# A diffusion-transformer step on one core: the activation arena as sixteen tensors, early products P1 ahead of P2, and a modulation moved to TensorE

## The chip, the cores and the metric

The kernel runs on one core of one Trainium2 chip. The metric is device time in microseconds (us) of one execution. A run has one number, and a kernel's time is the median of its runs.

## The reference, cut to what matters

One inference step with two layers (DEPTH = 2), D = 1024, 1024 sample tokens and 128 context tokens, all in float32. Each layer normalises x, modulates it with a scale and a shift, projects it into three parallel branches (a convolution, grouped-query attention, neighbourhood attention), projects the branches back, and then runs a squared-ReLU MLP with 4096 hidden features.

```python
def _modulation(cvec, w, b):
    m = (jax.nn.silu(cvec) @ w + b)[:, None, :]
    return jnp.split(m, 6, axis=-1)

def _layer(x, mod, lw, ctx):
    sh1, sc1, g1, sh2, sc2, g2 = mod
    h = _rms(x, n1) * (1 + sc1) + sh1
    ...                                   # h @ w_in, convolution, two attentions
    x = x + g1 * (jnp.concatenate([a_out, b_out, c_out], axis=-1) @ w_out)
    h = _rms(x, n2) * (1 + sc2) + sh2
    x = x + g2 * (jnp.square(jax.nn.relu(h @ w1)) @ w2)
```

The modulation is `silu(c) @ ada_w + ada_b`, with ada_w of 1024 x 6144, for two conditioning vectors. The next layer's first third (shift and scale of its first norm) is needed when that layer begins.

## The kernel before, in words

Activations are kept feature by feature: a block has 128 features on the partitions and tokens along the row. The 1152 tokens are two halves of HT = 576 (512 sample and 64 context tokens each). Every float32 operand of a large matmul is split into a rounded part `hi` and a rest `lo`, and a product is the three matmuls hi*hi, hi*lo, lo*hi (`three`, L1369, on two PSUM banks of 288 columns).

**The arena.** One region of on-chip memory, 16 x 1152 words a partition, holds activations in split form, and at other times raw weights. It is one tensor under two names: `HA` (the type of split operands) and `HF` (plain float32). The order of all work is written out by hand, and a tile framework places the semaphores from the accesses it sees, so that an instruction waits for those before it whose data it needs or overwrites. Uses of the arena, in order: in the prologue, ada_w and half of the sample (HF); the normalised input `h` of a layer's first half (HA, `h_views`); the three branches' outputs (HA, `c_block`, `c_put`); the MLP's operands B11, B21, T2, B22 and T1 (HA, `ha`, `block`), with the plain difference `raw` (HF) on the place where T2's `lo` comes; and the weights w2, in four regions A12, A11, A22, A21 (HF, `w2`, `load2`).

**The MLP's first product** is done by a seven-product scheme (Winograd's form of Strassen's) on 2 x 2 blocks. The hidden features come in 16 groups g; a group has the products P1 to P7, of 24 matmuls each. P1 = A11*B11 and P2 = A12*B21 need only tokens of the first half, so for g < EARLY = 8 they run in an *early stage*, while VectorE and ScalarE still prepare the second half (`norm2(L, 1, norms)`, stepped by `next(pre)` once or twice after each product). P1 and P2 of an early group accumulate in the same two banks `psa`: ScalarE copies P1 out (`s1`), then P2 is added and read out as h11 = relu(...)^2. Both are stored in `sd`. The *main stage* then runs P6, P5, P7, P3, P4 for the early groups and all seven for the others. The hidden values go to memory (`hd`), through `stores` and `keep(n)`, which issues all but the last n.

w1 blocks are loaded by `load1` (256 KB each) into T tiles, combined by `sums1`, and split by `split1`; `prepare(x + 1)`, `prepare(x + 2)` do that two products ahead. All loads and stores are issued on SyncE's (SP) queue in the order of the program. T tiles number 18, S tiles (X, `ev`, `low`, `hi34` and others) 18, U tiles 19, PSUM banks 8.

**Around it.** `out_proj` makes the output projection in blocks n of 128 features, first tokens' half t = 0, then t = 1. It stores x (`dy`) through its own `keep`, runs `norm2` of the first half in between, and calls `M.begin`, which loads and splits the first w1 blocks. In the last group (g = 15), w2 loads are issued after each product from P2 on. Then come the steps of the second product: each takes `ti` (two hidden blocks, loaded from `hd`), and splits it and a w2 block.

**The next layer's first modulation.** In layer 0, `modulation_beside` runs beside the main stage as `fill`, stepped after every second product: VectorE multiplies and accumulates ada_w with the two conditioning vectors (tiles `macc`), and TensorE only sums over partitions. The other modulations (`modulation`) use TensorE: per 128 input features four matmuls with two columns of weights, into four strips of one bank `psmod`, and in the end four transposes (`psmt`).

At the end of layer 0, the next layer's first norm writes `h` into the arena (partly from GpSimd) beside the last w2 steps, which read HF.

Of the kernel before, what the change touches and what calls it, by code (L numbers as in the profile page):

```python
# [31 lines left out]
EARLY = 8  # L32
# [13 lines left out]
def hybrid_step(ctx, tc, I, O, depth=DEPTH):  # L46
# [23 lines left out]
    def h_views():  # L70

        return {si: tuple(HA[:, o:o + KT * SEGS[si][1]].rearrange("p (k c) -> p k c", k=KT) for o in two)
                for si, two in enumerate(((4096, 8192), (0, 12288), (16384, 17408)))}

    def c_block(x, kt):

        return HA.rearrange("p (r x k c) -> p x k r c", r=2, x=2, k=KT)[:, x, kt]
# [33 lines left out]
    HA, HF = (nc.alloc_sbuf_tensor_at(n, [128, 16 * NT], dt, offset=ARENA)[:, :] for n, dt in (("HA", F32R), ("HF", F32)))  # L111
# [68 lines left out]
    def modulation(l, groups, first=False):  # L180
# [4 lines left out]
        def fetch():  # L185
            if todo:
                r, k = todo.pop(0)
                cols = slice(r * 2048, (r + 1) * 2048)
                if first:
                    if k % 2 == 0:  # L190
                        o = {0: 0, 2: 12288, 4: 4096, 6: 8192}[k]
                        aw = HF[:, o:o + 4096].rearrange("p (a b) -> p a b", a=2)
                        ready.extend([aw[:, 0], aw[:, 1]])
                    load(ready[-2 + k % 2], I["ada_w"][l, k * 128:(k + 1) * 128, cols])
                    return
# [16 lines left out]
        for r in groups:  # L212
# [4 lines left out]
            for k in range(KT):  # L217
                aw = ready.pop(0)
                for j in range(4):
                    a = aw[:, j * 512:(j + 1) * 512] if first else aw[j]  # L220
                    mm(ps[32 * j:32 * j + 2, :], silc[:, k, :], a, start=(k == 0), stop=(k == KT - 1))
                if not first:
                    fetch()
                yield
# [16 lines left out]
            yield  # L241

    def modulation_beside(l, rs):

        todo = [(r, k, b) for r in rs for k in range(KT) for b in range(2)]
        ready = []

        def fetch():
            if todo:
                r, k, b = todo.pop(0)  # L250
                aw = T([512], n="aw")
                c = r * 1024 + b * 512
                load(aw, I["ada_w"][l, k * 128:(k + 1) * 128, c:c + 512])
                ready.append(aw)

        fetch()
        fetch()
        yield
        for r in rs:
            acc = [T([2, 256], n="macc") for _ in range(4)]  # L260
            for k in range(KT):
                for b in range(2):
                    aw = ready.pop(0)
                    for j in range(2):
                        x = aw[:, j * 256:(j + 1) * 256]
                        for s in range(2):
                            a = acc[2 * b + j][:, s, :]
                            if k == 0:
                                ts(a, x, silc[:, k, s:s + 1], ALU.mult)
                            else:  # L270
                                stt(a, x, silc[:, k, s:s + 1], a, ALU.mult, ALU.add)
                    fetch()
                    yield
            ps = P("psmod")
            nc.vector.memset(ps, 0.0)
            for _ in range(3):
                yield
            for j in range(4):
                mm(ps[32 * j:32 * j + 1, :], ones[:, 0:1], acc[j].rearrange("p s c -> p (s c)"), start=True, stop=True)
            mt = T([512], n="mt")  # L280
            nc.vector.tensor_copy(mt, ps)
            yield
            pt = P("psmt")
            for b in range(4):
                nc.tensor.transpose(pt[:, b * 128:(b + 1) * 128], mt[:, b * 128:(b + 1) * 128], ident)
            ptv = pt.rearrange("p (s b j x) -> p s j b x", s=2, b=2, j=4, x=32)
            for s in range(2):
                tt(mod[l][:, s, r * 8:(r + 1) * 8].rearrange("p (j b) -> p j b", j=4), ptv[:, s, :, :, 0],
                   ada_b(l)[:, r * 8:(r + 1) * 8].rearrange("p (j b) -> p j b", j=4), ALU.add)
                if r in (1, 4):  # L290
                    a, g = ((A1, n1g), (A2, n2g))[r == 4]
                    stt(a[l][:, s, :], mod[l][:, s, r * 8:(r + 1) * 8], 1.0, g(l), ALU.add, ALU.mult)
            yield
# [41 lines left out]
    def norm_out(parts, hi, lo):  # L335

        late = None
        for k in range(KT):
            way, jobs, c = NORM_WAYS[k], [], 0
            for si, rb, A, B in parts:  # L340
                n = SEGS[si][1]
                t = (T if n > 128 else U)([n], n="nx")
                jobs.append((t, hi[:, k, c:c + n], lo[:, k, c:c + n], xs(k, si), rb, A[:, k:k + 1], B[:, k:k + 1], partial(like, si)))
# [48 lines left out]
    def prologue(pr):  # L392
# [10 lines left out]
        xh = HF[:, 8192:12288].rearrange("p (a b) -> p a b", a=4)  # L403
        for i in range(4):
            load(xh[:, i, :], I["x_sample"][(i + 4) * 128:(i + 5) * 128, :])
# [1598 lines left out]
```

## Time and profile before

| what | value |
|---|---|
| median of 3 runs | 3122.18 us (3115.1 to 3123.33) |
| the profiled execution's own time | 3122.03 us |
| its span, first to last instruction | 3120.3 us |
| mean granted TensorE clock | 0.959 |
| busy: TensorE / VectorE / ScalarE / GpSimd | 92% / 68% / 45% / 21% |
| early stage, layer 0 and layer 1 | 754.5 to 849.2 us, 2307.7 to 2402.6 us |
| last five products of w1, layer 0 and layer 1 | 1161.7 to 1198.1 us, 2695.9 to 2731.0 us |

PE is TensorE, PEld its weight loads, DVE VectorE, ACT ScalarE, POOL GpSimd, SP SyncE (here: the queue that issues DMAs). In rows of waits, the first name is the engine that sat idle with the tile it was about to write, and behind the arrow stands what ended the wait; then total us, count, longest. In rows of groups, a count follows the x, then busy us and mean ns of one, then idle us just before them. In the timeline the start and the duration come first, and idle time before the row stands in brackets. In rows of stretches: start and end, length, then busy us of each engine with the number of its instructions, the granted clock, the DMA engines' share and GB/s. Most instructions are recorded in helpers: L97 is `tt` (VectorE, or GpSimd), L94 is `acopy` (ScalarE), L91 is `act`, L100 is `stt`, L141 is `load`.

### The profile page before, as it was taken

Reading aid. Unit: us, or ns where it says so; the run is one execution under the profiler, and the core shown is the slowest. Engines: PE = TensorE matmul, PEld = TensorE weight load, DVE = VectorE, ACT = ScalarE, POOL = GpSimd, SP = SyncE. Lnnn points to the kernel's source line nnn. Section 1 sums busy time; section 2 is a strip of 40 time slices with the busy share of each in tenths; the row PEclk is TensorE's granted clock in tenths of the full one; section 3 lists DMA queues with packets and bytes.
Section 4 is the critical chain, followed back from the end, with each engine's and each line's share of the span. In section 5 each row is a group of like instructions: output and inputs, shape, how many; then the busy total and the mean of one; then the engine's idle time right before and its main releaser. Section 6 shows DMA issues by size and latency. Waiting matters only on the chain.

```text
span 3120.3 us, 52813 instructions
## 1 busy us (share of the span) xinstructions
PE 2881.6 (92%) x20284; PEld 2561.1 (82%) x20284; DVE 2132.6 (68%) x4113; ACT 1395.5 (45%) x2864; POOL 655.6 (21%) x595
## 2 busy tenths in 40 slices
PE   6998999998799997999889998999988999889999
PEld 4888645898699987999878785458977999879998
DVE  6587777845687763858575877778466766376576
ACT  4334366844444443333452343568344444334343
POOL 3576256300000000000225762563000000000000
PEclk7999999999899998999989998999998999999999
DMA  7377202333465547453433670033333654374434
GB/s 274 95 193 196 66 16 77 89 106 108 135 216 194 170 145 258 131 168 96 129 127 94 186 218 31 16 96 90 103 111 128 197 179 142 121 259 164 131 99 160
DMA packets 422974, 430.42 MB, mean 138 GB/s; under 512 B 119873, under 2 KB 299841, under 8 KB 421697
## 3 DMA queue, kind: packets, MB, share of 16 engines
q1 hardware_dynamic: 422720, 427.04, 43.8%
q8 instruction: 160, 2.62, 0.3%
q14 instruction: 94, 0.76, 0.1%
HBM read 298.50 MB, written 128.45 MB: 137 GB/s over the span
## 4 chain that ended last, share of the span: by engine, by line
PE 72%; DVE 14%; DMA 5%; ACT 4%; issue 2%; POOL 2%; SPq 1%; DVEq 0%; ACTq 0%; POOLq 0%
PE ps L1369 20%; PE psa L1369 9%; PE psc L1369 6%; PE pso L1369 5%; PE psb L1369 5%; PE psacc L1168 3%; PE pspv L1035 2%; PE pspt L1019 2%; PE pst L591 2%; DVE cacc L100 2%; PE pst L592 2%; PE pst L593 2%; PE psst L1182 2%; PE psm L1094 1%; PE psd L1369 1%
## 5 line engine op out<-in xcount | busy, mean ns | idle before, releaser
L1369 PE MATMUL ps<-ts,w2h 128*128 128x288 f32 x3584 | 634.6, 299 | 43.5 <-ACT w2h L94 32.4
L1369 PEld LDWEIGHTS ps<-ts,w2h 128*128 128x128 f32 x3584 | 532.0, 191 | 50.0 <-ACT w2h L94 39.5
L1369 PE MATMUL ps<-ts,w2l 128*128 128x288 f32 x1792 | 386.4, 297 | 3.4 <-DVE w2l L97 3.4
L94 ACT CAST ts<-ti 128x576 fp32r<-128x576 f32 x256 | 172.2, 673 | 324.5 <-PE ps L1369 204.7
L591 PE MATMUL pst<-wh,HA 128*128 128x256 f32 x1040 | 297.5, 286 | 0.0
L1369 PEld LDWEIGHTS ps<-ts,w2l 128*128 128x128 f32 x1792 | 290.9, 191 | 4.3 <-DVE w2l L97 4.2
L592 PE MATMUL pst<-wl,HA 128*128 128x256 f32 x1040 | 293.9, 283 | 0.0
L593 PE MATMUL pst<-wh,HA 128*128 128x256 f32 x1040 | 293.6, 282 | 0.0
L1369 PE MATMUL psa<-HA,w1h 128*128 128x288 f32 x1024 | 200.1, 320 | 66.4 <-DVE HF L97 32.2
L91 ACT ACTIVATE ev<-ev 128x576 f32<-128x576 f32 x192 | 131.9, 687 | 253.6 <-DVE ev L97 250.6
L97 DVE TENSOR_TENSOR ts<-ti,ts 128x576 fp32r<-128x576 f32 x256 | 195.9, 765 | 68.3 <-ACT ts L94 68.3
L100 DVE SCALAR_TENSOR_TENSOR X<-ps,mod,X 128x288 f32<-128x288 f32 x336 | 112.1, 409 | 172.4 <-PE ps L1369 172.4
L1369 PEld LDWEIGHTS psa<-HA,w1h 128*128 128x128 f32 x1024 | 166.2, 207 | 76.7 <-DVE HF L97 33.5
L591 PEld LDWEIGHTS pst<-wh,HA 128*128 128x128 f32 x1040 | 198.1, 190 | 19.1 <-issue 7.8
L97 POOL TENSOR_TENSOR nacc<-nacc,nsq 128x512 f32<-128x512 f32 (+1 forms) x12 | 18.9, 1577 | 889.0 <-ACT nsq L91 889.0
L593 PEld LDWEIGHTS pst<-wh,HA 128*128 128x128 f32 x1040 | 198.4, 191 | 0.0
L592 PEld LDWEIGHTS pst<-wl,HA 128*128 128x128 f32 x1040 | 198.3, 191 | 0.1
L1793 POOL COPY yu<-X 128x128 f32<-128x128 f32 x8 | 5.6, 719 | 898.3 <-ACT ts L94 861.4
L1369 PE MATMUL pso<-HA,woh 128*128 128x288 f32 x1024 | 177.3, 295 | 0.0
L1096 DVE TENSOR_REDUCE mx<-psm 128x1 f32<-128x384 f32 x288 | 142.3, 547 | 33.6 <-PE psm L1094 33.5
L91 ACT ACTIVATE pt<-psst 128x512 f32<-128x512 f32 x216 | 118.4, 597 | 94.5 <-PE psst L1183 93.6
L97 DVE TENSOR_TENSOR w1l<-w1r,w1h 128x512 fp32r<-128x512 f32 x128 | 87.0, 689 | 105.1 <-ACT w1h L94 105.1
(283 smaller groups left out, 7108.5 us busy)
## 6 DMA issues: line engine op xcount, KB each, us to landing
ti<-hd SPq DMA_DIRECT2D x128, 576.0 KB, 3.9
hd<-ev SPq DMA_DIRECT2D x224, 288.0 KB, 3.7
aw<-in_ada_w SPq DMA_DIRECT2D x160, 256.0 KB, 4.0
w1r<-in_mlp_w SPq DMA_DIRECT2D x160, 256.0 KB, 4.1
HF<-in_mlp_w SPq DMA_DIRECT2D x128, 256.0 KB, 4.4
ddA<-o SPq DMA_DIRECT2D x144, 128.0 KB, 3.0
wr<-in_w_in SPq DMA_DIRECT2D x28, 512.0 KB, 4.1
qd<-ddA SPq DMA_DIRECT2D x48, 256.0 KB, 3.4
```

What stands on the lines that cost most here:

```text
L91: nc.scalar.activation(out=out, in_=in_, func=func, scale=scale, bias=bias, **k)
L94: nc.scalar.copy(out, in_)
L97: (eng or nc.vector).tensor_tensor(out=out, in0=a, in1=b, op=op)
L100: nc.vector.scalar_tensor_tensor(out=out, in0=a, scalar=s, in1=b, op0=op0, op1=op1)
L591: mm(o, hi, wh, start=(k == 0), stop=False)
L592: mm(o, hi, wl, start=False, stop=False)
L593: mm(o, lo, wh, start=False, stop=(k == KT - 1))
L1019: nc.tensor.transpose(ps[0:n, c], self.p[j][:, o:o + n], ident)
L1035: mm(ps[64 * j:64 * j + 64, 0:128], v[j], self.at[j, i], start=(i == 0), stop=(i == nb - 1))
L1096: nc.vector.tensor_reduce(out=mx[j][:, qt, b:b + 1], in_=ps[:, 0:384], op=ALU.max, axis=AX.X)
L1168: mm(acc[64 * j:64 * j + 64, :], v, pt[:, j, :], start=(kt == 0), stop=(kt == 8))
L1369: mm(ps[h][:, 0:HH], x, y[:, h * HH:(h + 1) * HH], start=(start and z == 0), stop=(stop and z == 2), skip_group_check=True)
```

## The change

1. `HA` and `HF` become lists of sixteen tensors of 1152 columns, the i-th of both at the same place. Each use names the tensor it touches. The regions of w2 move to tensor borders (two blocks of 512 columns in each tensor). `h` of the context tokens now lies in the last 128 columns of the sixteen tensors; branch outputs of context tokens, which lie half in one tensor and half in another, are written in two pieces; the prologue's loads of ada_w are halved in size and doubled in number.
2. In the early stage P1 runs LEAD = 3 products ahead of P2. P1 and P2 have separate banks (`psa`, `psd`). P2's result is added to `s1` by VectorE, and then squared by ScalarE (Relu, Square over 576 columns). w1 blocks are loaded and split one at a time by `load_next` and `begin_next`, a split two products and a load five products ahead. `M.begin` starts its splits after the last block of the output projection. The last store of x moves from ahead of the remaining begin steps to after norm2's third step.
3. The main stage's w1 loads for group g + 1 are issued at P5 (before: at P6 for early groups, at P2 for the others). Loads for group 0 come six products ahead of the early stage's end.
4. `modulation_beside` is gone; `modulation(l + 1, [0])` takes its place, stepped at every fourth product from group 8 on.

```diff
-EARLY = 8
+EARLY, LEAD = 8, 3
...
-    HA, HF = (nc.alloc_sbuf_tensor_at(n, [128, 16 * NT], dt, offset=ARENA)[:, :] for n, dt in (("HA", F32R), ("HF", F32)))
+    HA, HF = ([nc.alloc_sbuf_tensor_at(f"{n}{i}", [128, NT], dt, offset=ARENA + 4 * NT * i)[:, :] for i in range(16)]
+              for n, dt in (("HA", F32R), ("HF", F32)))
...
     def c_put(si, kt, o, n):
         if si < 2:
-            return tuple(c_block(x, kt)[:, si, o:o + n] for x in range(2)) + ((lambda a: a),)
-        return tuple(c_block(x, kt)[:, :, 512:HT] for x in range(2)) + ((lambda a: a.rearrange("p (r c) -> p r c", r=2)),)
+            return [tuple(c_block(x, kt, si)[:, o:o + n] for x in range(2)) + (slice(0, n),)]
+        return [tuple(c_block(x, kt, t)[:, 512:HT] for x in range(2)) + (slice(64 * t, 64 * t + 64),) for t in range(2)]
...
     # out_proj, at its end
-        keep()
         run(begin)
         run(g0)
         yield "rest"
-        yield from norm2(L, 1, norms)
+        for i, _ in enumerate(norm2(L, 1, norms)):
+            if i == 2:
+                keep()
+            yield
...
     def ha(o, i, at=HA):
-        return at[:, o + i * HT:o + (i + 1) * HT]
+        return at[o + i // 2][:, i % 2 * HT:i % 2 * HT + HT]
...
     # Mlp
         def begin(self):
-            self.load1(0, ("A11", "A12"))
-            yield
-            self.load1(1, ("A11", "A12"))
-            self.split1(0, "A11")
-            self.split1(0, "A12")
-            yield
-            self.split1(1, "A11")
-            self.split1(1, "A12")
+            self.seq = [(g, "A11") for g in range(LEAD)]
+            for g in range(EARLY):
+                self.seq += [(g, "A12")] + [(g + LEAD, "A11")] * (g + LEAD < EARLY)
+            self.loaded = self.split = 0
+            for _ in range(3):
+                self.load_next()
+                yield
+            for _ in range(2):
+                self.begin_next()
+                yield
...
+        def begin_next(self):
+            self.load_next()
+            if self.split < len(self.seq):
+                self.split1(*self.seq[self.split])
+                self.split += 1
...
     # mlp
         def w2(b, gi):
-            return HF[:, region[b] + gi * 512:region[b] + (gi + 1) * 512]
+            return HF[region[b] + gi // 2][:, gi % 2 * 512:gi % 2 * 512 + 512]
...
         def chain_of(g, p):
             if p in ("P5", "P3"):
                 return "c"
-            return ("a" if p in ("P1", "P2") else "b") if g < EARLY else "d" if p == "P2" else "a"
+            return "d" if p == "P2" else "a" if p == "P1" or g >= EARLY else "b"
...
     # taken
-                elif p == ("P2" if early else "P4"):
+                elif p == "P4" and not early:
                     act(to, x, ACTF.Relu)
                     tt(to, x, to, ALU.mult)
                 else:
-                    tt(to, x, (s1[:, c] if p == "P6" else to), ALU.add)
+                    tt(to, x, (s1[:, c] if p in ("P2", "P6") else to), ALU.add)
             if p == "P2":
+                squared(h11)
                 if early:
                     stores.append((sd[l][g], e1.rearrange("p a c -> p (a c)")))
-                else:
-                    squared(h11)
                 stores.append((hd[l][0, g], h11))
...
-        M.load1(2, ("A11", "A12"))
-        seq = [(g, p) for g in range(EARLY) for p in ("P1", "P2")]
+        seq = [(g, "P1") for g in range(LEAD)]
+        for g in range(EARLY):
+            seq += [(g, "P2")] + [(g + LEAD, "P1")] * (g + LEAD < EARLY)
         for x, (g, p) in enumerate(seq):
-            if p == "P1":
-                if g + 2 < EARLY:
-                    M.split1(g + 2, "A11")
-                    M.split1(g + 2, "A12")
-                if g + 3 < EARLY:
-                    M.load1(g + 3, ("A11", "A12"))
-                if g == EARLY - 2:
-                    M.load1(0, ("A11", "A21", "A22", "A12"))
+            M.begin_next()
             product(g, p)
             keep(2)
             next(pre, None)
             if x % 4 == 3:
                 next(pre, None)
+            if x == len(seq) - 6:
+                M.load1(0, ("A11", "A21", "A22", "A12"))
             if x == len(seq) - 2:
                 M.sums1(0)
...
-            if p == ("P6" if g < EARLY else "P2") and g + 1 < NG:
+            if p == "P5" and g + 1 < NG:
                 M.load1(g + 1, ("A11", "A21", "A22", "A12"))
...
-            if x % 2:
+            if g >= EARLY and x % 4 == 0:
                 next(fill, None)
...
-            m = mlp(L, M, out, iter(()) if last else modulation_beside(l + 1, (0, 1)), last)
+            m = mlp(L, M, out, iter(()) if last else modulation(l + 1, [0]), last)
```

More of the change, by code (lines that the diff above doesn't have):

```diff
@@ L187, in fetch @@
                 r, k = todo.pop(0)
-                cols = slice(r * 2048, (r + 1) * 2048)
                 if first:
                     if k % 2 == 0:
[L191 to L194, printed above, removed]
+                        o = {0: 0, 2: 12, 4: 4, 6: 8}[k]
+                        ready.extend([[HF[o + 2 * a + b][:, c:c + 512] for b in range(2) for c in (0, 512)] for a in range(2)])
+                    o = {0: 0, 2: 12, 4: 4, 6: 8}[k - k % 2] + 2 * (k % 2)
+                    for b in range(2):
+                        c = r * 2048 + b * 1024
+                        load(HF[o + b][:, 0:1024], I["ada_w"][l, k * 128:(k + 1) * 128, c:c + 1024])
                     return
@@ L219, in modulation @@
                 for j in range(4):
-                    a = aw[:, j * 512:(j + 1) * 512] if first else aw[j]
-                    mm(ps[32 * j:32 * j + 2, :], silc[:, k, :], a, start=(k == 0), stop=(k == KT - 1))
+                    mm(ps[32 * j:32 * j + 2, :], silc[:, k, :], aw[j], start=(k == 0), stop=(k == KT - 1))
                 if not first:
@@ L240, in modulation @@
                     stt(A2[l][:, s, :], mod[l][:, s, 32:40], 1.0, n2g(l), ALU.add, ALU.mult)
-            yield
[L243 to L257, printed above, removed]
-        yield
[L259 to L269, printed above, removed]
-                            else:
[L271 to L292, printed above, removed]
             yield
@@ L402, in prologue @@
         load(vecs[0], I["vecs"][0])
-        xh = HF[:, 8192:12288].rearrange("p (a b) -> p a b", a=4)
+        xh = [HF[8 + i][:, 0:1024] for i in range(4)]
         for i in range(4):
-            load(xh[:, i, :], I["x_sample"][(i + 4) * 128:(i + 5) * 128, :])
+            load(xh[i], I["x_sample"][(i + 4) * 128:(i + 5) * 128, :])
         xp = [T([512], n="xtp") for _ in range(2)]
@@ L581, in stat @@
             c = 0
[L582 removed]
+        return a[k][:, c:c + 128], b[k][:, c:c + 128]
     def tok_group(L, t, nt, w):
@@ L1045, in end @@
             tt(cc, self.ps[:, 0:128], self.rb, ALU.mult)
-            chi, clo, see = c_put(self.si, kt, self.o, 128)
-            acopy(chi, see(cc))
-            tt(clo, see(cc), f32(chi), ALU.subtract, nc.gpsimd)
+            for chi, clo, c in c_put(self.si, kt, self.o, 128):
+                acopy(chi, cc[:, c])
+                tt(clo, cc[:, c], f32(chi), ALU.subtract, nc.gpsimd)
     def gqa(L):
@@ L1670, in prepare @@
                 M.sums1(g)
-            if p in ("P1", "P6") and g < EARLY:
+            if p == "P6" and g < EARLY:
                 for b in ("A11", "A12"):
```

56 lines of the change are left out of this document (29 added, 27 removed).

## The prediction

> **What bounds the kernel now.** I read the page first: the busy shares, the slices with the granted clock, and the DMA issues.
>
> ```profile
> span 3120.3 us, 52813 instructions
> PE 2881.6 (92%) x20284; PEld 2561.1 (82%) x20284; DVE 2132.6 (68%) x4113; ACT 1395.5 (45%) x2864; POOL 655.6 (21%) x595
> PE   6998999998799997999889998999988999889999
> PEclk7999999999899998999989998999998999999999
> w1r<-in_mlp_w SPq DMA_DIRECT2D x160, 256.0 KB, 4.1
> HF<-in_ada_w SPq DMA_DIRECT2D x8, 1024.0 KB, 12.8
> ```
>
> TensorE bounds the kernel, with 239 us of idle time. The low digits of the PE row stand in pairs, one per layer. Next I asked what ended TensorE's idle time.
>
> ```profile
> PE psa L1369 <- DVE HF L97: 32.2, 6, 7.1
> PE psa L1369 <- ACT ev L94: 19.0, 16, 7.0
> PE psc L1369 <- DMA HF<-in_mlp_w: 14.8, 4, 4.1
> PE psa L1369 <- DMA HF<-in_mlp_w: 11.5, 2, 5.8
> ```
>
> Columns are total, count, longest. The rows with HF are odd: these matmuls read HA (psa and psc are products of HA blocks), never HF. P1 and P2 read B11 and B21 (the first half of HA), while VectorE writes `raw` in the HF range of T2. So a write through one name holds up reads through the other wherever they lie. Inside HA there is no such wait: norm2 writes B11/B21 while the output projection reads HA, and 640 to 754.5 below has no idle TensorE. Third, the stretches by stage (PE, PEld, DVE, ACT, POOL busy, clock, DMA).
>
> ```profile
> 640.00:754.50 114.50, 114.50 (x911) 111.92 (x910) 54.43 (x131) 41.55 (x95) 3.72 (x10) 1.00 0.35 105
> 754.50:849.20 94.70, 66.21 (x390) 61.42 (x388) 58.38 (x107) 43.52 (x96) 0.00 (x0) 0.82 0.35 117
> 2307.70:2402.60 94.90, 66.19 (x391) 61.41 (x390) 58.52 (x107) 43.59 (x96) 0.00 (x0) 0.82 0.34 116
> 780.10:849.20 69.10, 49.91 (x295) 46.66 (x293) 44.11 (x77) 32.65 (x72) 0.00 (x0) 0.83 0.34 116
> 849.20:1161.70 312.50, 299.29 (x2208) 293.76 (x2208) 242.58 (x482) 135.83 (x256) 0.00 (x0) 0.99 0.57 186
> 2402.60:2695.90 293.30, 292.14 (x2184) 289.40 (x2184) 191.64 (x344) 134.58 (x256) 0.00 (x0) 1.00 0.52 169
> 1161.70:1198.10 36.40, 23.31 (x121) 22.70 (x120) 4.47 (x9) 7.13 (x14) 0.00 (x0) 0.72 0.31 103
> 2695.90:2731.00 35.10, 21.82 (x121) 21.13 (x120) 4.53 (x9) 7.19 (x14) 0.00 (x0) 0.81 0.33 106
> 1525.00:1575.00 50.00, 35.09 (x198) 31.13 (x197) 39.43 (x60) 24.22 (x45) 21.21 (x10) 0.85 0.52 165
> ```
>
> They are: output projection; early products of layers 0 and 1 (16 each); the rest of the early stage after the second-half rstd; the main w1 stage of layer 0 (with the modulation on VectorE beside it) and of layer 1 (without); the last five products of w1, twice; the turn into layer 1. Fourth, the chain and the timeline inside the early stage.
>
> ```profile
> 746.71 1.29 DVE w1l L97 x2
> 754.96 1.29 DVE w1l L97 x2
> 760.97 0.80 DVE X L100 x2
> 767.31 5.39 PE psa L1369 x24
> 772.71 1.03 PE psn L326 x4
> 853.56 3.17 PE psc L1369 x24
> ```
>
> A product of 24 matmuls takes 3.17 us on a warm TensorE and 5.39 after an idle time of 7. Sixteen warm products are 50.7 us; the stage takes 94.7.
>
> **The change, part by part.** The sum is made against the profiled execution: 3122.0 us, 1.7 above its span and 0.2 below the median of 3122.18.
>
> *Last five products of w1.* With sixteen tensors, the loads of w2 into HF0 to HF7 meet only HA0 to HA7 (B11, B21), whose last readers, P1 and P2 of the last group, are done. The five products become 5 x 3.17 = 15.9 us. Gain 36.4 - 15.9 = 20.5 and 35.1 - 15.9 = 19.2, together 39.7. Of the 36.4, 13.1 are the three DMA waits and the rest is TensorE restarting slowly. What is late next is the first w2 step:
>
> ```profile
> 1200.35 2.16 SPq L141 DMA_DIRECT2D HF<-in_mlp_w  x4
> 1202.56 0.43 SPq L141 DMA_DIRECT2D ti<-hd  x1
> 1209.06 0.67 ACT L94 CAST ts<-ti 128x576 fp32r<-128x576 f32 x1 [10.33 <-DMA ti<-hd]
> 1210.30 1.33 PE L1369 MATMUL ps<-ts,w2h 128*128 128x288 f32 x4 [12.19 <-ACT w2h L94]
> ```
>
> Its input ti is queued on SP behind the last hidden stores, which wait for P4's evacuation, and four weight loads. The diff leaves that order, so I keep the 12.2 us. Bounds per layer: 15 if the bunched loads slow ti by 5, 25 if ti comes earlier because fewer loads are still in flight.
>
> [...]
>
> *Early stage.* Removed: the four HF waits and P2's wait for ScalarE to copy P1 out of the shared bank. Added: P2 has its own banks; VectorE adds s1 in place of a multiply, ScalarE does Relu and Square on 576 columns in place of Relu twice on 288:
>
> ```profile
> L97 DVE TENSOR_TENSOR ev<-psb,ev 128x288 f32<-128x288 f32 x96 | 39.3, 451 | 30.6 <-PE psb L1369 22.1 <-DMA ev<-sd 8.5
> L97 DVE TENSOR_TENSOR ev<-psa,ev 128x288 f32<-128x288 f32 x96 | 39.4, 452 | 68.4 <-ACT ev L91 50.3 <-PE psa L1369 18.1
> 1162.48 1.40 ACT L91 ACTIVATE ev<-ev 128x576 f32<-128x576 f32 x2 [2.81 <-DVE ev L97]
> 826.49 0.71 ACT L91 ACTIVATE ev<-psa 128x288 f32<-128x288 f32 x2 [2.12 <-PE psa L1369]
> 759.90 0.42 PE L1369 MATMUL psa<-HA,w1l 128*128 128x288 f32 x2
> 800.26 0.76 DVE L97 TENSOR_TENSOR HA<-HF,HA 128x576 fp32r<-128x576 f32 x1 [0.79 <-ACT HA L94]
> L97 DVE TENSOR_TENSOR w1l<-w1r,w1h 128x512 fp32r<-128x512 f32 x8 | 5.2, 686 | 0.0
> ```
>
> VectorE pays nothing more, ScalarE 8 x 0.7 = 5.6 us, and its Relu now waits for VectorE, so casts queued behind it come later. A loss too: the first w1 split is no longer made inside the output projection; it is queued behind the last update of X (760.97). Two pairs of splits that stood ahead of it (1.29 us each) are gone, so update 758.5, squares, cast and subtraction let P1 of group 0 start at about 760.9, cold, where before it ended at 760.3. Then 5.4, two products, psn 1.0, and P2 of group 0: 760.9 + 5.4 + 6.3 + 1.0 + 3.2 = 776.8. From there TensorE alone would need 12 products, to 815. VectorE has 44.1 us (row 780.1 to 849.2) plus one evacuation 0.8, three more splits at 0.65 (5.2 over 8) and that of S2: 47.6, to 824.4 without a pause. Its pauses: four T2 subtractions that wait 0.8 for their cast (3.2) and, in the second half, five squares that hold ScalarE's casts about 1 us each (5). P6 of group 0 starts at about 832 instead of 849.2: 17 us per layer, 34 in all. Ends per layer: 34 (TensorE's 815) and 5 (each of the eight squares laid whole on VectorE's chain, 11, plus 1 for tile slots: up to five `ev` live in place of two). I take 17 since VectorE's busy time is the nearest row. The last store of X moves past the w1 loads on SP, so these are early; nobody waits for that store but norm2's in-place scaling 20 us later. The w1 loads of later groups move one or two products down, behind no other store than one that is ready.
>
> *Modulation on TensorE.* The first row goes out, with 16 shorter instructions, and the other two give the price of what comes in, 8 groups of 8 matmuls and 4 transposes:
>
> ```profile
> L100 DVE SCALAR_TENSOR_TENSOR macc<-aw,silc,macc 128x256 f32<-128x256 f32 x112 | 46.6, 478 | 0.0
> 140.71 1.04 PE L221 MATMUL psmod<-aw,silc 128*2 128x512 f32 x8
> 242.59 1.09 PE L230 MATMUL psmt<-ident,mt 128*128 128x128 f32 x4 [6.12 <-DVE mt L226]
> ```
>
> Without the VectorE work layer 0's main stage falls from 312.5 to layer 1's 293.3, 19.2 us. Then 8 x 1.04 + 1.09 = 9.4 come back; the 6.12 wait has four products between copy and transpose to hide it now. The net gain is 19.2 - 9.4 = 9.8; ends 0 (each group waiting 1.2 us more for weights) and 11.
>
> *Turn into layer 1.* TensorE idles 14.9 of 50 us, and part is this:
>
> ```profile
> POOL HA L97 <- DVE w2l L97: 8.6, 2, 5.8
> ```
>
> GpSimd writes HA while VectorE reads HF elsewhere. VectorE is 79% busy there, so I take 5; ends 0 and 12.
>
> *Small things.* Eight 1 MB loads become sixteen (8 x 0.54 = 4 us more of SP by the HF row above, beside landings of 12.8): 0, ends -1 and 3. The context columns are written in two pieces, some 16 short instructions a layer beside a busy TensorE: cost 1, ends 0 and 3.
>
> Sum: 39.7 + 34 + 9.8 + 5 - 1 = 87.5, so 3122.0 - 87.5 = 3034.5.
>
> **The rivals.** *Covered:* the elementwise work keeps up and the early stage falls to TensorE's 815, 34 us a layer: 3000. For it: VectorE is idle for 36 of 94.7 us today. Against: after 777 it has 47.6 us for TensorE's 38. [...]
>
> *Bound moved:* squares behind adds, casts behind squares; 5 a layer: 3058, and 3068 where nothing is left of it.
>
> *Nothing is separated:* the waits still follow the whole arena. Then only P2's 7 us wait per layer and the modulation go: 3122 - 14 - 9.8 = 3098. Against: the waits by name.
>
> *Slower:* w1 weights late. Their four loads (2.2 us to issue, 4.1 to land) now start at P5; four sums at 0.69 and the S2 split, 1.3, need 4.1 more (estimated from the split rows), 10.4 of the four products' 12.7. If landings took 5.2 us longer, all 30 groups would lose 2.9 us and eat the whole gain; at 5.7, 3.4 us each, 3137. Against: SP runs through the two products it moves past without waiting.
>
> **How the numbers follow.** Forecast 0.58 (its own range 3015 to 3055), covered 0.15, bound moved 0.16, nothing separated 0.06, late weights 0.05. The range 2998 to 3074 leaves out the last two and the edges. About 0.3% (9 us) can be told from no change: faster 0.93, same 0.03, slower 0.04.
>
> **What would show it.** No wait of a psa or psc matmul for HF; five last products in 16 us; some 12 us still before w2; P6 of group 0 about 77 us after the output projection's end, with VectorE over 70% busy; layer 0's main w1 stage at 303. It is wrong if HF waits remain, or if the early stage stays above 90.

## Result and profile after

The changed kernel takes 3046.05 us (median of 4 runs, 3043.01 to 3049.24), the kernel before beside it 3120.52 (3115.1 to 3123.33): a ratio of 0.9764, 95% interval 0.9745 to 0.9782. Forecast were 87.5 us of gain; the medians give 74.5 and the two profiled spans, 3120.3 and 3042.1, give 78.2. In the rows of the changed kernel the helpers stand on other lines than before: L99 is `tt`, L96 `acopy`, L93 `act`, L102 `stt`, L144 `load` and L1319 `three`. The page of the changed kernel:

```profile
span 3042.1 us, 52749 instructions
PE 2857.0 (94%) x20328; PEld 2538.6 (83%) x20328; DVE 2082.6 (68%) x3985; ACT 1404.7 (46%) x2880; POOL 655.7 (22%) x607
PE   6998999999799998999889999999997999899999
PEclk7999999999899998999999999999998999999999
```

TensorE's idle time is 185 us, it was 239. Of the pairs of low slices, the one at the end of w1 is less deep: it holds an 8 in each layer, before it held a 7 in layer 0 and two 8 in layer 1. What ended the idle times (total, count, longest):

```profile
PE ps L1319 <- ACT w2h L96: 29.1, 5, 11.9
PE psa L1319 <- ACT w1h L96: 22.0, 8, 6.0
PE psb L1319 <- ACT w1h L96: 16.8, 2, 8.4
```

No psa or psc matmul waits for HF any more. New is a wait of 6 us at the first early product and one of 8.4 us at the first late product (psb is P6's bank), once in each layer. Before, P6 waited 1.2 us there; the experiments below show 1.2 with the new arena alone and 8.0 with the new order alone, so the wait came with the order. The stretches that answer to those of before: early stage, main w1 stage with its last five products, and those five alone, for layer 0 and then layer 1; last the turn into layer 1.

```profile
754.40:836.20 81.80, 59.83 (x391) 56.56 (x389) 59.00 (x109) 49.48 (x98) 0.00 (x0) 0.89 0.41 134
836.20:1157.10 320.90, 320.28 (x2372) 309.63 (x2372) 197.46 (x356) 142.25 (x270) 0.00 (x0) 0.99 0.61 196
1141.20:1157.10 15.90, 15.90 (x121) 15.67 (x119) 4.48 (x9) 7.16 (x14) 0.00 (x0) 1.00 0.79 283
2257.00:2338.40 81.40, 59.55 (x391) 56.17 (x389) 58.91 (x108) 49.42 (x98) 0.00 (x0) 0.88 0.41 135
2338.40:2651.20 312.80, 310.91 (x2304) 307.74 (x2304) 195.73 (x350) 141.76 (x270) 0.00 (x0) 0.99 0.53 174
2635.30:2651.20 15.90, 15.90 (x121) 15.70 (x119) 4.51 (x9) 7.13 (x14) 0.00 (x0) 1.00 0.77 276
1483.00:1533.00 50.00, 36.91 (x211) 33.35 (x210) 39.53 (x64) 25.58 (x49) 21.47 (x10) 0.88 0.53 167
```

The five products now leave TensorE no idle time. The early stage is 13 us shorter in each layer, and VectorE's work in it is what it was (59.0 us, before 58.4), now at 72% of the time.

The table holds stage times in us, read off the traces: from the output projection's end to the first P6, from there to the last product of w1, from there to the first w2 matmul, and w2 itself (in layer 0 up to layer 1's projection). The kernels below the second row are those of the experiments. Stage times come from the one profiled run of each kernel. The medians were taken in groups, each with its own runs of the kernel before: 3115.8 beside arena_only, lead_only, no_fill and sq_behind, 3116.7 beside split_early, s2_early and ti_early, 3120.6 beside ti_three, three and four, 3119.2 beside x_late. Across groups, compare the ratios to before that stand with each experiment, not the medians.

| kernel | early, L0 / L1 | main w1, L0 / L1 | gap | w2, L0 / L1 | median |
|---|---|---|---|---|---|
| before | 94.9 / 94.9 | 348.9 / 328.4 | 12.2 / 13.2 | 390.9 / 368.5 | 3120.5 |
| after | 81.8 / 81.4 | 320.9 / 312.8 | 11.8 / 11.9 | 389.5 / 370.9 | 3046.1 |
| arena_only | 86.3 / 85.5 | 328.1 / 310.3 | 12.3 / 12.0 | 390.0 / 370.7 | 3065.9 |
| lead_only | 90.9 / 90.9 | 348.8 / 329.0 | 12.1 / 12.6 | 393.4 / 369.6 | 3114.7 |
| no_fill | 80.4 / 81.6 | 330.0 / 310.6 | 12.1 / 11.9 | 389.7 / 370.6 | 3055.8 |
| sq_behind | 77.8 / 77.5 | 319.4 / 311.9 | 11.8 / 11.6 | 389.5 / 371.2 | 3040.9 |
| split_early | 75.4 / 75.3 | 319.2 / 315.9 | 12.1 / 11.9 | 389.2 / 368.8 | 3034.4 |
| s2_early | 74.1 / 77.4 | 326.3 / 314.4 | 11.8 / 11.9 | 389.6 / 371.1 | 3047.3 |
| ti_early | 81.0 / 80.4 | 319.8 / 310.3 | 0.1 / 0.1 | 401.7 / 384.1 | 3046.8 |
| ti_three | 81.9 / 80.9 | 320.5 / 310.2 | 0.1 / 0.1 | 401.1 / 380.9 | 3044.3 |
| three | 72.1 / 72.9 | 320.6 / 311.1 | 0.1 / 0.1 | 399.3 / 381.4 | 3027.9 |
| four | 67.9 / 68.0 | 323.8 / 317.8 | 0.1 / 0.1 | 400.6 / 380.6 | 3026.5 |
| x_late | 71.7 / 72.9 | 320.8 / 312.1 | 0.1 / 0.1 | 400.9 / 381.8 | 3026.0 |

### The profile page after: what moved, and what is told of

Its sections match the earlier page's. It is cut to its first block, busy times and chain, and to the rows that moved or that the text cites. A ratio compares the mean times of both kernels' runs of the same rounds, so it can differ in the third digit from the quotient of the medians.

```text
span 3042.1 us, 52749 instructions
## 1 busy us (share of the span) xinstructions
PE 2857.0 (94%) x20328; PEld 2538.6 (83%) x20328; DVE 2082.6 (68%) x3985; ACT 1404.7 (46%) x2880; POOL 655.7 (22%) x607
## 4 chain that ended last, share of the span: by engine, by line
PE 71%; DVE 15%; DMA 4%; ACT 4%; issue 2%; POOL 2%; SPq 1%; DVEq 0%; ACTq 0%; POOLq 0%
PE ps L1319 21%; PE psa L1319 7%; PE psc L1319 6%; PE pso L1319 5%; PE psb L1319 5%; PE psacc L1118 3%; DVE cacc L102 2%; PE pspv L985 2%; PE pspt L969 2%; PE pst L541 2%; PE pst L542 2%; PE pst L543 2%; PE psst L1132 2%; PE psd L1319 2%; PE psm L1044 2%
## 5 line engine op out<-in xcount | busy, mean ns | idle before, releaser
L1319 PE MATMUL ps<-ts,w2h 128*128 128x288 f32 x3584 | 635.9, 299 | 42.7 <-ACT w2h L96 29.1
L1319 PEld LDWEIGHTS ps<-ts,w2h 128*128 128x128 f32 x3584 | 534.3, 191 | 48.7 <-ACT w2h L96 37.2
L1319 PE MATMUL ps<-ts,w2l 128*128 128x288 f32 x1792 | 387.5, 298 | 2.0 <-DVE w2l L99 2.0
L96 ACT CAST ts<-ti 128x576 fp32r<-128x576 f32 x256 | 172.0, 672 | 328.2 <-PE ps L1319 209.1
L1319 PEld LDWEIGHTS ps<-ts,w2l 128*128 128x128 f32 x1792 | 292.2, 191 | 2.4 <-DVE w2l L99 2.2
L93 ACT ACTIVATE ev<-ev 128x576 f32<-128x576 f32 x224 | 153.7, 686 | 279.1 <-DVE ev L99 275.6
L99 DVE TENSOR_TENSOR ts<-ti,ts 128x576 fp32r<-128x576 f32 x256 | 195.2, 762 | 68.0 <-ACT ts L96 68.0
L102 DVE SCALAR_TENSOR_TENSOR X<-ps,mod,X 128x288 f32<-128x288 f32 x336 | 112.1, 409 | 173.5 <-PE ps L1319 173.5
L541 PEld LDWEIGHTS pst<-wh,HA 128*128 128x128 f32 x1040 | 198.1, 191 | 19.2 <-issue 6.9
L99 POOL TENSOR_TENSOR nacc<-nacc,nsq 128x512 f32<-128x512 f32 (+1 forms) x12 | 18.9, 1577 | 848.7 <-ACT nsq L93 848.7
L99 DVE TENSOR_TENSOR w1l<-w1r,w1h 128x512 fp32r<-128x512 f32 x128 | 87.9, 690 | 137.1 <-ACT w1h L96 136.8
L1319 PE MATMUL pso<-HA,woh 128*128 128x288 f32 x1024 | 177.8, 295 | 0.0
L1319 PE MATMUL psa<-HA,w1h 128*128 128x288 f32 x768 | 141.0, 307 | 22.0 <-ACT w1h L96 22.0
L93 ACT ACTIVATE pt<-psst 128x512 f32<-128x512 f32 x216 | 118.1, 597 | 87.7 <-PE psst L1133 86.9
L99 POOL TENSOR_TENSOR R<-R,pt 128x1024 f32<-128x1024 f32 x60 | 149.3, 2489 | 24.4 <-ACT pt L93 22.4
```

Source lines behind the costliest of these rows:

```text
L93: nc.scalar.activation(out=out, in_=in_, func=func, scale=scale, bias=bias, **k)
L96: nc.scalar.copy(out, in_)
L99: (eng or nc.vector).tensor_tensor(out=out, in0=a, in1=b, op=op)
L102: nc.vector.scalar_tensor_tensor(out=out, in0=a, scalar=s, in1=b, op0=op0, op1=op1)
L541: mm(o, hi, wh, start=(k == 0), stop=False)
L1319: mm(ps[h][:, 0:HH], x, y[:, h * HH:(h + 1) * HH], start=(start and z == 0), stop=(stop and z == 2), skip_group_check=True)
```

## Experiments

### The three parts one by one

**arena_only** is the kernel before with the new views of the arena and nothing else (of the edit, the lines that make the tensors):

```diff
-    HA, HF = (nc.alloc_sbuf_tensor_at(n, [128, 16 * NT], dt, offset=ARENA)[:, :] for n, dt in (("HA", F32R), ("HF", F32)))
+    HA, HF = ([nc.alloc_sbuf_tensor_at(f"{n}{i}", [128, NT], dt, offset=ARENA + 4 * NT * i)[:, :] for i in range(16)]
+              for n, dt in (("HA", F32R), ("HF", F32)))
```

> The kernel before, with the arena as sixteen tensors and nothing else of the change (old order of the early products, modulation on VectorE). Theory 'whole-tensor waits': the last five products of w1 take 16 us in each layer instead of 36.4 and 35.1, no psa or psc matmul waits for HF, and the early stage of 94.7 us falls by most of its share of the HF waits (32.2 us over both layers) to about 82; 3120.5 - 40 - 25 - 1 = about 3055 us. Rival 'VectorE holds the early stage anyway': the last five products gain the same 40, the early stage stays at 90 or more because P2 still waits for the copy of P1 out of the shared bank: about 3075. Rival 'names do not matter': nothing moves, 3120.

Measured 3065.85 us, ratio to before 0.9837 (0.9822 to 0.9852). Its waits and stretches (early stage, last five products):

```profile
PE psa L1371 <- ACT ev L96: 41.4, 16, 7.2
755.20:841.50 86.30, 62.87 (x391) 59.09 (x390) 58.16 (x108) 43.36 (x96) 0.00 (x0) 0.84 0.38 128
1153.60:1169.50 15.90, 15.90 (x121) 15.71 (x119) 4.52 (x9) 7.11 (x14) 0.00 (x0) 1.00 0.79 280
```

The last five products gain all that was forecast, and no wait for HF is left. In the early stage, though, the 32.2 us of waits for HF did not go: psa's waits for ScalarE's copy of P1 rose from 19.0 to 41.4. In the timeline of layer 0 the three HF waits of 6.2, 2.8 and 7.1 us stand where this kernel has three of 5.1, 1.6 and 5.8 for the copy: each hid one for the shared bank. The stage gained 9, not the 12 that I expected: a value between the theory and its first rival.

**lead_only** is the kernel before with the other order, the separate banks and the moved loads, but one arena:

```diff
-            return ("a" if p in ("P1", "P2") else "b") if g < EARLY else "d" if p == "P2" else "a"
+            return "d" if p == "P2" else "a" if p == "P1" or g >= EARLY else "b"
...
-        seq = [(g, p) for g in range(EARLY) for p in ("P1", "P2")]
+        seq = [(g, "P1") for g in range(LEAD)]
+        for g in range(EARLY):
+            seq += [(g, "P2")] + [(g + LEAD, "P1")] * (g + LEAD < EARLY)
```

> The kernel before, with the new order of the early products, the separate banks, Relu and Square on ScalarE and the moved w1 loads, but one arena and the modulation on VectorE. Theory 'whole-tensor waits': the HF waits of the early stage and of the last five products stay (35 us there); without P2's waits for the copy of P1 the stage gains no more than 5 a layer: 3110 to 3120 us. Rival 'the order does it': the early stage falls to some 82 us without the sixteen tensors, 3095.

Measured 3114.69 us, 0.9993 (0.9983 to 1.0003): nothing that can be told from no change.

```profile
PE psa L1369 <- DVE HF L97: 30.9, 6, 7.0
PE psc L1369 <- DMA HF<-in_mlp_w: 14.8, 4, 4.0
761.40:852.20 90.80, 61.38 (x390) 59.79 (x389) 59.34 (x108) 49.47 (x98) 0.00 (x0) 0.83 0.37 121
```

The HF waits stand as before (32.2 and 14.8), and the stage gains 4. So in the early stage the order alone gives 4 a layer, the arena alone 9, and both together 13. The 8 us of both layers are not in the total. The profiled run was the slowest of the ten (3123.58 us), reached the early stage 7 us later than the kernel before, and took 2.5 and 1.1 us longer in w2; so its stages don't add up to the median, and where the 8 us went was not found.

**no_fill** is the changed kernel with the modulation back on VectorE, stepped after every second product as before:

```diff
-            m = mlp(L, M, out, iter(()) if last else modulation(l + 1, [0]), last)
+            m = mlp(L, M, out, iter(()) if last else modulation_beside(l + 1, (0, 1)), last)
```

> The changed kernel, with the next layer's first modulation back on VectorE as before. Theory 'VectorE bounds the w1 groups of layer 0': its main w1 stage goes from 320.9 us (first late P6 to the last product) back up by 9 or 10, and the total to about 3056. Rival 'VectorE now has room, since the waits for HF are gone': below 2 us, 3046 to 3048. Rival 'TensorE's cost is the larger': faster than the changed kernel, by up to 8.

Measured 3055.76 us, 0.9807 (0.9792 to 0.9821); layer 0's main stage takes 330.0 us, the changed kernel's 320.9. The modulation on TensorE is worth 9.1 us with the arena split, so VectorE's load does hold those groups (the ratios, 0.9807 and 0.9764, say 13 us in total, with some 7 of uncertainty):

```profile
839.20:1169.20 330.00, 317.75 (x2328) 312.98 (x2328) 245.92 (x488) 142.35 (x270) 0.00 (x0) 0.98 0.58 191
```

VectorE has 245.9 us of work here against 197.5 without the modulation. This kernel is also arena_only with the order added, and both were measured beside the same runs of before: 3065.85 and 3055.76. So the order with its moved loads, worth 1.1 us by itself (lead_only, not to be told from nothing), is worth 10.1 once the arena is split. The moved loads were not tried alone.

### What is left in the early stage

**sq_behind** moves Relu and Square of each early P2 behind the casts of the norm step:

```diff
             if p == "P2":
-                squared(h11)
                 if early:
-                    stores.append((sd[l][g], e1.rearrange("p a c -> p (a c)")))
...
+                    behind.append((g, e1, h11))
...
             if x % 4 == 3:
                 next(pre, None)
+            square_behind()
```

> The changed kernel; in the early products Relu and Square of P2's sum are issued behind the casts of the norm step of the same product, not ahead of them; same instructions, another order on ScalarE. Theory 'the squares hold ScalarE's casts': VectorE's pauses of 1.36 us at the low parts go, P6 of group 0 starts about 5 us earlier in each layer (836.2 to about 831), 3036 us. Rival 'VectorE's own work sets P6': P6 of group 0 moves by less than 1.5 us, 3046. Rival 'the tile ring': the squares' slots come free later and P1 waits for them: slower by 2 to 5 a layer.

Measured 3040.9 us, 0.9759 (0.9745 to 0.9774). ScalarE and VectorE of the changed kernel at one of the last low parts (tile `low`, the rests `lo` of the second half's operands):

```profile
809.91 1.40 ACT L93 ACTIVATE ev<-ev 128x576 f32<-128x576 f32 x2 [2.66 <-DVE ev L99]
811.21 0.66 ACT L96 CAST HA<-X 128x576 fp32r<-128x576 f32 x1
811.90 0.76 DVE L99 TENSOR_TENSOR low<-X,HA 128x576 fp32r<-128x576 f32 x1 [1.36 <-ACT HA L96]
```

and the same part in sq_behind:

```profile
815.96 0.67 ACT L96 CAST HA<-X 128x576 fp32r<-128x576 f32 x1
817.55 1.40 ACT L93 ACTIVATE ev<-ev 128x576 f32<-128x576 f32 x2 [0.35 <-DVE ev L99]
818.10 0.75 DVE L99 TENSOR_TENSOR low<-X,HA 128x576 fp32r<-128x576 f32 x1
```

In the first, Relu and Square wait 2.66 us for VectorE's sum, the cast stands behind them, and VectorE waits 1.36 us for that cast. In the second the cast is done before. The stage is 4.0 us shorter in each layer. Expected were 5, and in the total even the 4 can't be seen: 0.9759 of before, the changed kernel 0.9764. Split at VectorE's evacuation of P2 of group 0, the part behind it falls from 59.0 to 56.2 and 56.1 us, so 2.8 to 2.9 are the squares'; the part ahead of it, 22.9 and 22.4 in the changed kernel, is 21.6 and 21.4 here. That part scatters between 21.4 and 23.2 over the kernels that leave it alone.

**split_early** issues the first three loads of w1 at one step, so that the first two splits come ahead of the last update of X:

```diff
             for _ in range(3):
                 self.load_next()
-                yield
+            yield
             for _ in range(2):
                 self.begin_next()
                 yield
```

> The changed kernel; the first three loads of w1 are issued at one step of the output projection instead of three, so that the first two splits stand ahead of the last update of X, as such splits did before the change. Theory 'the start sets the whole stage': P1 of group 0 starts at the end of the output projection instead of 6.1 us behind it, the second half's rstd comes as much earlier, and P6 of group 0 moves by 5 to 6 us in each layer: 3035. Rival 'VectorE's work after the rstd sets the end, and the rstd hangs on the last update of X': P1 starts earlier, P6 of group 0 moves by less than 2 us: 3043 to 3046.

Measured 3034.39 us, 0.9729 (0.9715 to 0.9744): the largest single gain.

```profile
755.70:831.10 75.40, 59.05 (x391) 55.80 (x390) 58.89 (x108) 48.25 (x96) 0.00 (x0) 0.91 0.42 141
```

The part up to the first evacuation falls to 16.5 and 16.3 us, and the part behind it stays at 59.0 to a tenth, in both layers. So the 6.1 us that P1 of group 0 starts late pass whole into the end of the stage: the second half's rstd (the norm's factor, from the mean square) needs psn, TensorE's sum of the squares over the partitions, and psn is queued there behind the first two P1.

**s2_early** moves the sums and the S2 split of late group 0 three to four products forward:

```diff
-            if x == len(seq) - 6:
+            if x == len(seq) - 9:
                 M.load1(0, ("A11", "A21", "A22", "A12"))
-            if x == len(seq) - 2:
+            if x == len(seq) - 5:
                 M.sums1(0)
+            if x == len(seq) - 4:
...
+                M.split1(0, "S2")
```

> The changed kernel; the four weights of late group 0 are loaded, summed and S2 split three to four products earlier, ahead of the last low parts of the norm. Theory 'P6 of group 0 waits only for its own split, queued last': its wait of 8.4 us goes; the 3.4 us of sums and split on VectorE then stand ahead of the last early products, so P6 gains about 5 in each layer, and its first product is warm (2 more): 3032 to 3038. Rival 'what P5 and P7 need is as late': P6 starts earlier and the products behind it wait as long, under 2 us a layer: 3043 to 3046.

Measured 3047.32 us, 0.9774 (0.9758 to 0.9791): no gain. Waits of TensorE from the early stage's start to 860 us:

```profile
PE psa L1319 <- ACT w1h L96: 11.0, 4, 5.9
PE psc L1319 <- ACT w1h L96: 3.0, 1, 3.0
PE psb L1319 <- DVE ev L99: 2.1, 1, 2.1
```

P6 starts 7.7 and 4.0 us earlier, its wait of 8.4 is gone, and the products behind it wait instead: P5 (psc) for its split, P7 (psb) for VectorE's evacuation of P6. The main stage is 5.4 and 1.6 us longer, so that the two stages together gain 2.3 and 2.4, near the 2 of the rival, and the total gains nothing that can be seen. The rival holds; that VectorE's queue shifted and its work did not shrink is the likely reason, but only P7's wait for VectorE shows it.

### The gap before w2

**ti_early** and **ti_three** load one input, or three, ahead of the last hidden stores, and issue the first two or three steps' casts ahead of the last evacuation:

```diff
+            if x >= len(seq) - 3:
+                input_ahead(2 * (x - len(seq) + 3))
+            if x == len(seq) - 1:
+                ready2(0)
+                ready2(1)
+                ready2(2)
             product(g, p)
             keep(3)
```

> The changed kernel; the first input of the w2 stage is loaded ahead of the last hidden stores, and the first two steps' casts and splits are issued ahead of the last w1 product's evacuation. Theory 'order on SP': the 11.8 and 11.9 us from the last product of w1 to the first of w2 fall to 3 or less: 3028. Rival 'the stores in memory hold the load, not the queue' (the hidden blocks are one tensor in DRAM): the input still lands late, and the gap stays at 9 or more: 3043. Rival 'the next steps are as late': the first step starts early and the third waits, gain of half: 3036.

> The changed kernel; the first three inputs of the w2 stage (six steps) are loaded ahead of the last hidden stores, and the first three steps' casts and splits are issued ahead of the last w1 product's evacuation. With one input ahead the 12 us only moved to the third step. Theory 'order on SP and of the casts': each input queued behind the stores comes late, and with three of them ahead there is nothing left to wait for: 8 to 11 us a layer gained, 3024 to 3030. Rival 'VectorE and ScalarE are behind by the last group's sums and squares': the gap moves to the fourth step and the stage keeps its sum, 3046. Rival 'the weights of the first steps come late': psum steps wait for HF loads, 3040.

Measured 3046.8 us, 0.9769 (0.9754 to 0.9784), and 3044.32 us, 0.9757 (0.9743 to 0.9772). The gap of 12 us is gone in both, and w2 is as much longer. The first idle time of TensorE in w2, first with one input ahead, then with three:

```profile
1174.56 1.33 PE L1319 MATMUL ps<-ts,w2h 128*128 128x288 f32 x4 [8.73 <-ACT w2h L96]
```

```profile
1187.87 1.33 PE L1319 MATMUL ps<-ts,w2h 128*128 128x288 f32 x4 [7.09 <-ACT w2h L96]
1186.62 0.67 ACT L96 CAST ts<-ti 128x576 fp32r<-128x576 f32 x1 [20.82 <-DMA ti<-hd]
1180.00:1188.00 8.00, 0.91 (x7) 0.68 (x6) 0.68 (x1) 1.38 (x3) 0.00 (x0) 0.67 1.04 399
1188.00:1200.00 12.00, 9.46 (x51) 9.06 (x52) 8.80 (x17) 5.48 (x10) 0.00 (x0) 0.78 1.03 402
ti<-hd SPq DMA_DIRECT2D x9, 576.0 KB, 8.2
```

The wait moves to the first step whose input was not sent ahead. The last three rows show one reason: while TensorE stands idle the DMA engines are at a share of 1.04 and move 399 GB/s, they stay full up to 1200, and an input takes 8.2 us from issue to landing (3.9 over the whole changed kernel). None of the three things that I had expected names this. SP's queue in ti_three shows a second reason, which comes first in time and is part of what 'order on SP' said:

```profile
1153.32 11.58 SPq L144 DMA_DIRECT2D hd<-ev  x5
1164.95 5.08 SPq L144 DMA_DIRECT2D HF<-in_mlp_w  x10
1178.50 0.39 SPq L144 DMA_DIRECT2D ti<-hd  x1
SPq L144 <- DVE ev L99: 8.0, 2, 7.7
```

The fourth input, the one that TensorE waits for, is issued only at 1178.50, 18.9 us after the last product of w1 (1159.6). Ahead of it stand hidden stores, where SP waits 7.7 us for VectorE's results (the last row, taken from 1159 to 1182 us), and from 1165 on sixteen loads of weights, three more stores and two loads of X. The time from issue to landing is 8 of the 27 us between the last product and the landing.

**x_late** tests that with the three inputs and the two gains of the early stage kept:

```diff
-            if x < 8:
-                X[x] = S([2, HT], n="X")
-                load(X[x].rearrange("p t c -> p (t c)"), dy[l][:, x, :])
+            if x < 4 or 10 <= x < 14:
+                n = x if x < 4 else x - 6
+                X[n] = S([2, HT], n="X")
+                load(X[n].rearrange("p t c -> p (t c)"), dy[l][:, n, :])
```

> The kernel with squares behind the casts, the first splits early and three w2 inputs ahead; on top of it the loads of X[4] to X[7] (576 KB each), which w2 needs from its 32nd step on, are issued at steps 10 to 13 instead of 4 to 7. Theory 'the entry of w2 is bound by the DMA engines': between 1180 and 1200 us they stood at a share of 1.0 and 400 GB/s, and these 2.4 MB are 5.9 us of it, so the stage from the last w1 product to layer 1's projection falls from 399.4 by 4 to 6 and that of layer 1 (381.5) likewise: 3028 - 10 = about 3018 us. Rival 'the order on SP': the loads that remain wait as before, under 2 us a layer, 3025 or more.

```profile
1155.00:1176.00 21.00, 15.88 (x120) 15.64 (x118) 5.59 (x9) 0.91 (x2) 0.00 (x0) 1.00 1.02 363
1176.00:1184.00 8.00, 5.64 (x27) 5.65 (x28) 3.05 (x5) 3.41 (x7) 0.00 (x0) 0.57 1.04 392
1184.00:1190.00 6.00, 3.29 (x24) 3.02 (x22) 5.86 (x11) 6.00 (x12) 0.00 (x0) 0.97 1.04 405
1190.00:1192.00 2.00, 2.00 (x8) 1.79 (x8) 2.00 (x8) 0.64 (x2) 0.00 (x0) 0.50 0.76 302
1178.36 1.33 PE L1319 MATMUL ps<-ts,w2h 128*128 128x288 f32 x4 [7.48 <-ACT w2h L96]
```

Measured 3025.99 us (5 runs); w2 did not get shorter beside "three" (400.9 and 381.8 against 399.3 and 381.4). Counted from the last product of w1 (1149.8 here, 1159.6 in ti_three), the DMA engines are full up to about 42 us where it was 43. So the edit was a weak test: X[4] and X[5] were issued 4 to 5 us later than in "three", X[6] 9 us and X[7] 16 us, and only X[7] came behind the full stretch; later inputs moved up in their place. Besides, the input that TensorE waits for stands ahead of them on SP, issued 18.9 us after the last product as in ti_three, behind weights that were not moved. The rival's number came out. That the DMA engines are full when TensorE waits is shown (shares of 1.02 and 1.04), and that the awaited input is issued late too; whether fewer bytes ahead of it, or its place ahead of the stores, would end the wait was not tried and stays open.

### Together

"three" is sq_behind, split_early and ti_three in one; "four" has s2_early too; a first such kernel, all4, had ti_early in place of ti_three and early stages of 68.0 and 68.7 us.

> The changed kernel with squares behind the casts, the first splits early and three w2 inputs ahead. Theory 'separate waits add': early stage 81.6 - 4 - 6.3 = 71.3 us a layer and 8 to 11 before w2: 3046 - 20.6 - 19 = about 3006. Rival 'the inputs gain nothing': 3025. Rival 'the start and the squares overlap': early stage 74, 3012 with the inputs' gain.

> The same with S2 of late group 0 summed and split early as well. Theory 'VectorE's queue only shifts': early stage 68 a layer, but P7 waits 4 to 5 us longer for the evacuation of P6, so the total is within 4 us of the one without it: about 3004. Rival 'it adds': 3000 or less.

> The changed kernel with all of it: squares behind the casts, first splits early, S2 of late group 0 early, first w2 input early. Theory 'four separate waits': the early stage falls from 81.6 us to about 68 a layer and the gap before w2 to 3: 3046 - 27 - 18 = about 3001 us. Rival 'one bound under all': VectorE's 47.6 us of work after the second-half rstd is the floor of the early stage, and the gains overlap: early stage 74, total 3013. Rival 'no addition at all': 3028 or more.

Measured 3027.86 us (0.9701, 0.9684 to 0.9719), 3026.46 (0.9705, 0.9686 to 0.9724) and 3031.36 (0.9729, 0.9709 to 0.9749). The totals of 3001 to 3006 us that the theories named were missed by 22 to 30, since the 18 to 19 us expected from the gap before w2 did not come. The early stage's gains do add: 81.6 - 4.0 - 6.2 = 71.4, measured 72.1 and 72.9. With S2 early it is 68, as forecast, and P7's wait is there too:

```profile
PE psb L1319 <- DVE ev L99: 3.8, 1, 3.8
```

That row is of "four", and its main stage is 3.2 and 6.7 us longer than that of "three". The best median is that of x_late, 0.9701 (0.9687 to 0.9714) of the time before; "three" and "four" cannot be told from it. By the two ratios to before, x_late is at 0.9701 / 0.9764 = 0.9935 of the changed kernel.

## Why the prediction was right where it was, and where it was not

*Last five products: 39.7 forecast, 39.7 measured* (36.4 and 35.1 fell to 15.9 each). arena_only shows that the tensors alone do it. What follows the five products, the 12.2 us before w2, stayed at 11.8 and 11.9 as forecast. That it hangs on the input's place in SP's queue was half the story: ti_three shows full DMA engines behind it (a share of 1.04, 399 GB/s).

*Early stage: 34 forecast, 26.6 measured.* The first half of the working holds: P1 of group 0 at 760.6 (forecast 760.9), and VectorE's work after P2 of group 0 is the forecast 47.6:

```profile
776.60:836.20 59.60, 43.58 (x294) 41.03 (x292) 47.49 (x85) 38.56 (x74) 0.00 (x0) 0.90 0.42 144
```

The term that was mis-sized is that of the pauses: 8.2 us in the forecast (four of 0.8, five of 1.0), 59.6 - 47.5 = 12.1 here. VectorE's waits in this stretch are these: four low parts wait 1.36 or 1.37 for casts behind squares (forecast: five of 1) and two T2 subtractions 0.74 (forecast: four of 0.8). Together they are 6.9, not far from the forecast. What the working put at nothing are five splits of w1 that wait for their own casts, 3.5 together, the two longest behind ScalarE's activation of X, and 1.3 at the very end, where the S2 split waits behind the last pair of squares:

```profile
788.04 0.69 DVE L99 TENSOR_TENSOR w1l<-w1r,w1h 128x512 fp32r<-128x512 f32 x1 [1.34 <-ACT w1h L96]
836.19 1.29 DVE L99 TENSOR_TENSOR w1l<-w1S,w1h 128x512 fp32r<-128x512 f32 x2 [1.30 <-ACT w1h L96]
```

sq_behind gives 2.8 us of this part back. "Bound moved" named a mechanism that the trace shows, casts queued behind squares, at too high a price: with all pauses together the stage ended 4 us a layer later than forecast, not 12.

*The loss that I priced and let stand* was the larger one. That P1 of group 0 starts at about 760.9, because its split no longer stands ahead of the last update of X, costs 6.4 and 6.1 us net (split_early), half of what the stage gained.

*Covered* (3000) failed for the reason given against it: VectorE's 47.5 us for TensorE's 38. With all four edits the stage comes to 68 us, not to the 60 that the rival needs.

*Modulation: 9.8 forecast, 9.1 by no_fill.* The price of what comes in is 320.9 - 312.8 = 8.1 us against 9.4 forecast. Up to the last five products, layer 0's main stage fell from 312.5 to 305.0, by 7.5.

*Turn into layer 1: 5 forecast, 1.4 measured* over the whole w2 stage (390.9 to 389.5), and 1.8 of TensorE's work more in the 50 us (36.91, before 35.09). GpSimd's wait for w2l is gone; VectorE is as busy as before, 39.5 of 50 us. The false wait was not one that held TensorE: its own waits for GpSimd's writes of `h` (psf <- POOL HA, both layers) were 7.9 us and are 7.7.

*Not forecast:* layer 1 from its projection to the end of the output projection, whose work is the same but for the names of the tensors and some short pieces, took 8.0 us less; the last section says what is known of it. Layer 1's main stage gained 15.6 where its last five products alone gained 19.2. Of the 3.6 that are missing, 1.4 are P6 of group 0: it took 4.33 us at a granted clock of 1.00 and takes 5.73 at 0.55 after its wait of 8.4. The rest stays open; the whole stage takes 310.2 to 315.9 us in the eight kernels whose code for it is the same up to the last products (after, no_fill, sq_behind, split_early, ti_early, ti_three, three, x_late).

The two profiled spans differ by 78.2 us. The early stages give 26.6 of it, the last five products 39.7, the rest of the main stages 7.5 less 3.6, the gap before w2 1.7, w2 1.4 less 2.4, and the 8.0 of layer 1 that belong to no term of the working. By the spans the gain fell 9.3 us short of the forecast; without those 8.0 it would have been 17.3.

Of the marks that I set: no HF waits, five products in 16 us, 12 us before w2 and VectorE over 70% busy came out; P6 at 77 us came at 81.6; layer 0's main w1 stage, set at 303 up to the last five products, took 320.9 - 15.9 = 305.0. Late w1 weights and "nothing is separated" show in no row.

## What to carry to other kernels

When a false wait is removed, look for the true wait that stood under it: here 32 us of waits for one name turned into 22 us more of waits for a shared bank. Look at what stands in a queue behind an instruction that waits: here Relu and Square waited 2.66 us for VectorE's sum ahead of a cast, and VectorE waited 1.36 us for that cast; with them behind the casts the stage was 4.0 us shorter in each layer. A step moved earlier gained nothing here when what the next steps need came no earlier: sum the whole stage, not the gap that went.

## What the runs showed of the hardware

In the traces of before and after, the granted clock is 1.0 or 0.5 in every record. It is 0.5 in 37 stretches of the first and 27 of the second, of 3.4, 6.8, 10.2, 13.7 or 17.1 us, but for the last one of each trace, which reaches its end (2.3 and 4.3). After idle times of nearly the same length in the same code the clock was not the same: in the kernel before, TensorE idled 3.18 us ahead of 892.5 us, and the 3.4 us that followed were at 1.00; it idled 3.21 us ahead of 928.2 us, and 3.4 us at half speed began at 928.6. The stretch from layer 1's projection to its output projection's end, before and after:

```profile
1601.20:2307.70 706.50, 673.61 (x4643) 533.78 (x4642) 500.33 (x1002) 344.56 (x768) 300.17 (x276) 0.97 0.37 104
1558.50:2257.00 698.50, 666.79 (x4642) 529.22 (x4642) 499.14 (x1005) 343.72 (x774) 302.42 (x282) 0.98 0.38 106
```

The same matmuls take TensorE 6.8 us longer in the first (673.61 against 666.79). In this stretch the time at half clock was 41.0 us before and 23.9 after. In the profiled runs of the fourteen kernels the stretch took 698.1 to 706.6 us with 23.9 to 41.0 us at half clock: 0.44 us more for each us of it (correlation 0.87). The same stretch of layer 0 took 704.2 to 714.8 us with 34.1 to 53.4 (0.50, correlation 0.95). Among the twelve kernels with sixteen tensors, whose code in the stretch is the same but for the first loads and splits of w1, it took 698.1 to 704.0 us in layer 1 and 704.2 to 714.8 in layer 0. So from profile to profile this stage differed by 5.9 and 10.6 us without a change of its work, and a difference of that size need not be an effect of a change.

Whether the sixteen tensors have a part in the 8.0 us stays open. The two kernels with one arena, before and lead_only, are the two longest of the fourteen in layer 1 (706.6 and 705.0), and lead_only is so with no more time at half clock (30.7) than arena_only, ti_three and four, which took 699.9 to 701.3. In layer 0 the two lie among the others (705.3 and 712.9).
